# A squared-ReLU trunk on one core: a second block of each MLP up product computed with the input standing still, and PSUM taken in pairs of banks

## The chip, the cores and the metric

The kernel runs on one core of a Trainium2 chip. Its engines have short names in the profile: PE (TensorE, matmuls), PEld (its weight loads), DVE (VectorE), ACT (ScalarE), POOL (GpSimd) and SP (SyncE, whose queue carries the weight DMAs here). The metric is the device time of one execution in microseconds (us), lower is better; the number compared is the median of several runs.

## The reference

Two layers work on 256 tokens of 2048 channels, in float32. Layer 0 mixes tokens with a convolution module, layer 1 with latent attention. Each is followed by the MLP that the change is about:

```
def rms_norm(x, g):
    y = xf * lax.rsqrt(jnp.mean(xf * xf, axis=-1, keepdims=True) + NORM_EPS)
    return (y * g).astype(x.dtype)

def sq_relu_mlp(h, w1, w2):
    return jnp.square(jax.nn.relu(h @ w1)) @ w2

h = rms_norm(x, norm_mlp_g[layer])
x = x + sq_relu_mlp(h, mlp_w1[layer], mlp_w2[layer])
```

The weight `mlp_w1` is 2048 x 8192 and `mlp_w2` is 8192 x 2048. A final norm follows layer 1.

## The kernel before, in words

**Three products for one.** Each float32 number is split into an upper part that TensorE's fast float32r form holds exactly (`hi`, a copy by ScalarE) and the rest (`lo`, a subtraction by VectorE). A product is hi x hi + lo x hi + hi x lo, three matmuls (`mm3`, L202 to 206). Weights come by DMA into `raw` (three buffers), are split into `hi` and `lo` tiles (`upper_half` L165, `lower_half` L174, six buffers each) and are used once, so that VectorE and ScalarE work a few units ahead of TensorE and no further.

**The MLP** (`mlp`, L624) goes through the 8192 hidden columns in two halves (`hf`). A half is an up product into eight groups `g` of 512 columns, then a down product from them into the 2048 channels. The activations of group `g` stay in SBUF as `gh`/`gl` (or `sh`/`sl`) tiles.

**The up product has two forms.** In the form with the weight standing still (L754 to 765) 128 x 128 blocks of the weight are the stationary operand, and the input of all 256 tokens moves past: one matmul of 512 columns takes `hi` of the weight against both parts of the input side by side (`xt`), one of 256 columns takes `lo` of the weight against the input's upper part. A group is 128 matmuls in four units of four k-blocks, into four PSUM banks; the result is channel-major, as the down product wants it. The group's close (L776 to 787) adds the two halves of each bank, squares the positive part, multiplies by the square of the norm's scale (`r2_row`) and splits the result.

In the form with the input standing still (`up_block`, L697) the input's 128 x 128 blocks are stationary and 512 weight columns move. There the 2 x 2 blocks of a pair of k-blocks can be multiplied with seven products in the place of eight (`Sums.mixed` L551, Strassen's method as Winograd wrote it): 21 matmuls for a pair and not 24 (`Sums.plain`, L564). Seven combinations of weight blocks are made by `mixed_weights` (L491), seven of the input by `up_forms` (L650, tiles `fh`/`fl`). The sums need eight banks: four that are results (`e`) and four that are joined at the end (`u`, by `parts`, L587). The result is token-major: it is scaled and made positive by ScalarE (L715), turned by 16 transposes on TensorE (L724), squared (L727) and split. The turning is kept back and run among the matmuls of the group behind the block (`late`, L768).

Before the change a half runs the groups 0 to 3 with the weight standing still, then one block for the groups 4 and 5, then 6 and 7 (`UP_AT = 4`). Of the block's eight pairs the pairs 1, 2, 3 and 4 are mixed, in the order 0, 1, 2, 5, 3, 4, 6, 7; its plain pairs take their stationary operand from `xt`.

**The down product** (L788 on) has the activations stationary and the weights moving, with seven or eight of its sixteen pairs mixed (`MIXED`, L44), in two sweeps of 1024 columns with the eight banks changing roles.

**What sets the order.** The convolution and the attention are in an order written out by hand. In the MLP a planner orders each engine's instructions by their place in the program and by when it thinks that they are ready; TensorE's matmuls come in the order of the program. A PSUM or SBUF tile is given out again when all that read it are done.

Of the kernel before, what the change touches and what calls it, by code (L numbers as in the profile page):

```python
# [80 lines left out]
def trunk_kernel(  # L81
# [33 lines left out]
    psum, psum_cx = {}, [ExitStack()]  # L115

    def repool(name, **banks):

        psum_cx[0].close()
        psum_cx[0] = ExitStack()  # L120
        psum.clear()
        for kind, n in banks.items():
            psum[kind] = psum_cx[0].enter_context(tc.tile_pool(name=kind + name, bufs=n, space=PSUM, reuse_waits="tile"))
# [21 lines left out]

    def acc_tile():
        return psum["acc"].tile([P, NB], F32, tag="acc", name=nm("acc"))
# [372 lines left out]
    def mixed_inputs(v, fh, fl):  # L520

        def halves(src, at, n):
            hi, lo = fh[:, at : at + n, :], fl[:, at : at + n, :]
# [3 lines left out]
        a = v.rearrange("p k (t n) -> p (k t) n", t=T)  # L529
        a11, a21, a12, a22 = (a[:, i, :] for i in range(4))  # L530
        halves(a[:, 0:1, :], 0, 1)
        halves(a[:, 2:4, :], 1, 2)
        mixed_sums(a11, a21, a12, a22)
        halves(a, 3, 4)

    class Sums:


        def __init__(self, n, by_dma, swap=None):
            self.n, self.by_dma = n, by_dma  # L540
            ps = [acc_tile() for _ in range(8)]
            e, self.u = (ps[:4], ps[4:])[:: -1 if (n > 0 if swap is None else swap) else 1]
            self.e = [e[2 * t : 2 * t + 2] for t in range(T)]
# [80 lines left out]
    def mlp(layer, ssq, next_gain, finish=None, before=None, beside=None, after_up=None):  # L624

        with ExitStack() as cx:
# [4 lines left out]
            r2_row = mp.tile([P, S], F32, name=nm("r2_row"))  # L631
            repool(f"mlp{layer}", acc=8)

            def v_tile():
                return mp.tile([P, 2, S], F32, tag="v", name=nm("v"), bufs=4)

            def room():
                return v_tile().rearrange("p a n -> p (a n)")

            def scales():  # L640
                r = rms_rstd(ssq[:, :, :NNB], NNB, D, "n")
                r2 = small.tile([P, T], F32, tag="r2", name=nm("r2"))
                nc.vector.tensor_tensor(r2, r, r, op=ALU.mult)
                o = [acc_tile() for _ in range(4)][0]
                for t in range(T):
                    nc.tensor.transpose(o[:, t * P : (t + 1) * P], r2[:, t : t + 1].broadcast_to([P, P]), ident)
                nc.scalar.activation(r2_row, o[:, :S], AF.Copy)
                return r

            def up_forms(i, fs):  # L650

                p, v = UP_MIXED[i], v_tile()
                xp = xt[p // 2][:, 2 * p % 4 : 2 * p % 4 + 2, :].bitcast(F32)
                nc.vector.tensor_tensor(v, xp[:, :, :S], xp[:, :, S:], op=ALU.add)
                a = v.rearrange("p k (t n) -> p (k t) n", t=T)
                a11, a21, a12, a22 = (a[:, j, :] for j in range(4))
                mixed_sums(a11, a21, a12, a22)
                h, l = (f[i // 2][:, i % 2, 3:, :] for f in fs)
                nc.scalar.activation(h, a, AF.Copy)
                nc.vector.tensor_tensor(l, a, h.bitcast(F32), op=ALU.subtract)  # L660
                for c, f in enumerate(fs):
                    o = f[i // 2][:, i % 2]
                    nc.scalar.activation(o[:, 0, :], xp[:, 0, c * S : c * S + P], AF.Copy)
                    nc.scalar.activation(o[:, 1:3, :], xp[:, 1, c * S : (c + 1) * S].rearrange("p (t n) -> p t n", t=T), AF.Copy)

            def up_form(k, fs):

                i = UP_MIXED.index(k // 2)
# [6 lines left out]
            def activations(g, b2, v):  # L675

                gh, gl = gs[g]
                if 2 * g + b2 in ms:
                    mixed_inputs(v, gh[:, b2], gl[:, b2])
                    return  # L680
                if g in mixed:
                    v = v.rearrange("p k (t n) -> p (k t) n", t=T)
                    h, l = gh[:, b2, : 2 * T, :], gl[:, b2, : 2 * T, :]
                else:
                    h, l = (a[:, 2 * b2 : 2 * b2 + 2, :] for a in (gh, gl))
                nc.scalar.activation(h, v, AF.Copy)
                nc.vector.tensor_tensor(l, v, h.bitcast(F32), op=ALU.subtract)
# [9 lines left out]
            def up_block(hf, g, fs, temps):  # L697
# [3 lines left out]
                left = [p for p in UP_ORDER if p in UP_MIXED]  # L701
                for p in UP_ORDER:
                    if p in UP_MIXED:
                        left.remove(p)
                        sums.mixed(mlp_w1[layer], 2 * p, up_form(2 * p, fs), not left)
                        continue
                    end = p == UP_ORDER[-1]
                    if end:
                        parts = sums.parts(*temps)
                    sums.plain(mlp_w1[layer], 2 * p, xh_kt, xl_kt, 2 * p, end)  # L710
                for c in range(2):
                    for t in range(T):
                        z = parts[t, c]
# [1334 lines left out]
```

## Time and profile before

| | |
|---|---|
| median of 3 runs | 1932.62 us (1932.3 to 1933.16) |
| the profiled execution: its own time | 1932.2 us |
| its span, first to last instruction | 1930.4 us |
| PE / PEld busy | 99% / 86% of the span |
| DVE / ACT / POOL busy | 87% / 59% / 13% |
| HBM read over the span | 189 GB/s |

The profile is of one execution. A row of the groups gives line, engine, operation, output and inputs, count, busy time and mean duration; a row of the windows gives a stretch from the span's start, its length, and the busy time and number of instructions of each engine in it (an instruction that reaches in from outside is counted too). The ends of matmuls are modelled, and a matmul's row overlaps the next one's: what a matmul costs is read from the length of a stretch with a known number of them.

### The profile page before, as it was taken

Reading aid. Unit: us, or ns where it says so; the run is one execution under the profiler, and the core shown is the slowest. Engines: PE = TensorE matmul, PEld = TensorE weight load, DVE = VectorE, ACT = ScalarE, POOL = GpSimd, SP = SyncE. Lnnn points to the kernel's source line nnn. Section 1 sums busy time; section 2 is a strip of 40 time slices with the busy share of each in tenths; the row PEclk is TensorE's granted clock in tenths of the full one; section 3 lists DMA queues with packets and bytes.
Section 4 is the critical chain, followed back from the end, with each engine's and each line's share of the span. In section 5 each row is a group of like instructions: output and inputs, shape, how many; then the busy total and the mean of one; then the engine's idle time right before and its main releaser. Section 6 shows DMA issues by size and latency. Waiting matters only on the chain.

```text
span 1930.4 us, 28294 instructions
## 1 busy us (share of the span) xinstructions
PE 1916.9 (99%) x10485; PEld 1665.0 (86%) x10485; DVE 1675.8 (87%) x2602; ACT 1147.1 (59%) x1752; POOL 248.7 (13%) x208
## 2 busy tenths in 40 slices
PE   9999999999999999999999999999999999999998
PEld 8999888888888888888898998888888888888887
DVE  7999989997989789799976765898889988888998
ACT  5667756565555655655576655565655556565554
POOL 6999200000010100000001420000000010000000
PEclk9999999999999999999999999999999999999999
DMA  7766455656585865655656545464646686465774
GB/s 230 214 183 189 153 188 189 212 175 197 177 247 198 249 211 172 208 175 197 218 173 178 142 132 187 162 212 158 220 162 222 217 249 220 163 228 175 231 219 150
DMA packets 222235, 375.48 MB, mean 195 GB/s; under 512 B 16392, under 2 KB 107792, under 8 KB 221840
## 3 DMA queue, kind: packets, MB, share of 16 engines
q1 hardware_dynamic: 216448, 363.28, 57.6%
q0 software_dynamic: 4320, 7.87, 2.2%
q10 hardware_dynamic: 1328, 2.52, 0.4%
q8 instruction: 82, 1.34, 0.3%
q14 instruction: 57, 0.47, 0.1%
HBM read 363.68 MB, written 2.10 MB: 189 GB/s over the span
## 4 chain that ended last, share of the span: by engine, by line
PE 96%; DVE 2%; DMA 0%; issue 0%; ACT 0%; ACTq 0%; DVEq 0%
PE acc L764 18%; PE acc L206 18%; PE acc L204 18%; PE acc L205 18%; PE acc L765 10%; PE acc L925 8%; PE acc L1389 2%; DVE sum L1012 1%; DMA xs<-in_x 0%; PE acc L1637 0%; PE acc L1666 0%; PE acc L1668 0%; PE acc L1638 0%; PE acc L1639 0%; PE acc L1667 0%; PE tr L268 0%
## 5 line engine op out<-in xcount | busy, mean ns | idle before, releaser
L171 ACT ACTIVATE hi<-raw 128x1024 fp32r<-128x1024 f32 (+2 forms) x542 | 545.8, 1032 | 235.9 <-PE acc L764 105.8
L175 DVE TENSOR_TENSOR lo<-raw,hi 128x1024 fp32r<-128x1024 f32 (+2 forms) x477 | 560.6, 1194 | 127.9 <-ACT hi L171 120.9
L764 PE MATMUL acc<-xt,hi 128*128 128x512 f32 x1536 | 534.3, 391 | 0.0
L498 ACT ACTIVATE hi<-raw 128x1024 fp32r<-128x1024 f32 (+1 forms) x312 | 288.2, 948 | 303.4 <-DVE raw L506 164.7
L765 PE MATMUL acc<-xt,lo 128*128 128x256 f32 x1536 | 433.0, 282 | 0.0
L499 DVE TENSOR_TENSOR lo<-raw,hi 128x1024 fp32r<-128x1024 f32 (+1 forms) x312 | 332.6, 1087 | 45.0 <-ACT hi L498 40.3
L764 PEld LDWEIGHTS acc<-xt,hi 128*128 128x128 f32 x1536 | 288.3, 188 | 60.4
L765 PEld LDWEIGHTS acc<-xt,lo 128*128 128x128 f32 x1536 | 290.3, 189 | 0.3
L204 PE MATMUL acc<-hi,sh 128*128 128x512 f32 x514 | 200.1, 389 | 0.0
L206 PE MATMUL acc<-lo,sh 128*128 128x512 f32 x514 | 200.0, 389 | 0.0
L204 PE MATMUL acc<-hi,gh 128*128 128x512 f32 (+1 forms) x516 | 200.0, 388 | 0.0
L205 PE MATMUL acc<-hi,gl 128*128 128x512 f32 (+1 forms) x516 | 199.9, 387 | 0.0
L206 PE MATMUL acc<-lo,gh 128*128 128x512 f32 (+1 forms) x516 | 199.9, 387 | 0.0
L925 PE MATMUL acc<-xt,hi 128*128 128x256 f32 x1024 | 180.2, 281 | 0.3 <-ACT b L1208 0.2
L205 PE MATMUL acc<-hi,sl 128*128 128x512 f32 x450 | 175.1, 389 | 0.0
L583 POOL DMA_DIRECT2D xs<-v x30 | 26.3, 957 | 1135.4 <-DVE lo L175 701.9
L1012 DVE SCALAR_TENSOR_TENSOR sum<-ub,w_dw,sum 128x256 f32<-128x256 f32 x409 | 164.4, 485 | 3.6 <-ACT sum L982 3.0
L175 POOL TENSOR_TENSOR lo<-raw,hi 128x1024 fp32r<-128x1024 f32 x65 | 154.8, 2404 | 17.2 <-ACT hi L171 17.2
L925 PEld LDWEIGHTS acc<-xt,hi 128*128 128x128 f32 x1024 | 154.6, 188 | 1.1 <-ACT xt L1192 0.6
L925 PE MATMUL acc<-xt,lo 128*128 128x256 f32 x512 | 139.2, 279 | 0.0
L206 PEld LDWEIGHTS acc<-lo,gh 128*128 128x128 f32 x516 | 96.9, 188 | 19.9
L204 PEld LDWEIGHTS acc<-hi,gh 128*128 128x128 f32 x516 | 96.9, 188 | 19.7
(342 smaller groups left out, 3083.6 us busy)
## 6 DMA issues: line engine op xcount, KB each, us to landing
raw<-in_mlp_w SPq DMA_DIRECT2D x255, 1024.0 KB, 5.5
raw<-in_conv_w_pw SPq DMA_DIRECT2D x62, 512.0 KB, 5.1
raw<-in_conv_w_pw SPq DMA_DIRECT2D x16, 1024.0 KB, 5.0
raw<-in_mla_w_o SPq DMA_DIRECT2D x16, 1024.0 KB, 5.3
raw<-in_mla_w_kv_up SPq DMA_DIRECT2D x32, 256.0 KB, 3.9
xs<-v POOLq DMA_DIRECT2D x30, 256.0 KB, 7.6
raw<-in_mla_w_in SPq DMA_DIRECT2D x8, 576.0 KB, 3.7
raw<-in_mla_w_in SPq DMA_DIRECT2D x4, 1024.0 KB
```

The costliest lines, as they stand in the source:

```text
L171: nc.scalar.activation(hi, raw[:, js, :], AF.Copy)
L175: eng.tensor_tensor(lo, raw, hi.bitcast(F32), op=ALU.subtract)
L204: nc.tensor.matmul(ps, sh, mh, start=start, stop=False)
L205: nc.tensor.matmul(ps, sl, mh, start=False, stop=False)
L206: nc.tensor.matmul(ps, sh, ml, start=False, stop=stop)
L498: nc.scalar.activation(hi, src, AF.Copy)
L499: nc.vector.tensor_tensor(lo, src, hi.bitcast(F32), op=ALU.subtract)
L764: nc.tensor.matmul(ps[b], wh[:, bs], xhl(k), start=k == 0, stop=False)
L765: nc.tensor.matmul(ps[b][:, :S], wl[:, bs], xh(k), start=False, stop=k == KC - 1)
L925: nc.tensor.matmul(pss[c][b][:, :S], w[i][:, bs], (xh, xl)[j](k), start=k == i + j == 0, stop=end and k == k0 + nk - 1 and (i, j) == terms ...
L1012: nc.vector.scalar_tensor_tensor(out=out, in0=ubs[c][:, w : w + S], scalar=tap(c, w), in1=base, op0=ALU.mult, op1=ALU.add)
L1389: nc.tensor.matmul(ps2[b][t], x_kt(k, t), w[:, bs], start=k == g == i == 0, stop=k == KC - 1 and i == len(group) - 1,)
```

## The change

- Each half of an up product now has two blocks with the input standing still, for the groups 0 and 1 and for 2 and 3; the groups 4, 5, 6 and 7 keep the weight standing still. The order is 4, 5, block, 6, block, 7 (`UP_PLAN`). The mixed pairs of the down product move to the groups 0 to 3; their number stays.
- The mixed pairs of a block are 2, 3, 4 and 5, in the order 0, 2, 3, 1, 4, 5, 6, 7. Both blocks of a half use the same input forms, made once, two pairs by one call.
- The plain pairs take the input from copies of `xt[0]` and `xt[3]`, made by ScalarE into buffers that later hold activations (`up_copies`). The second block has the copy of `xt[3]` only; the buffer of the other is needed by then.
- PSUM in the MLP is given out in pairs of banks (`pair_tile`). A group's close is one copy and one addition of two banks each, one instruction for positive part and scale, a square by ScalarE, and the split, each over 1024 elements. The scale is that of the norm (`r_row`), the small tiles `r2` are gone, and it is turned by TensorE inside the last unit of the first group rather than behind it.
- The sums of a block are joined and made positive two banks at a time; the 16 transposes of a block run in one piece, and its squares and splits are twice as wide.
- The tables of the rotary embedding (`beside`) are made in layer 0's second half, not its first. At the start of the attention four small writes that touch PSUM tiles come behind the first three products.

```diff
-MIXED = {(layer, half): (0, 1, 4, 5, 8, 9, 12) + (13,) * (layer + half < 2) for layer in range(2) for half in range(2)}
+MIXED = {(layer, half): tuple(range(7 + (layer + half < 2))) for layer in range(2) for half in range(2)}
-UP_AT, UP_ORDER, UP_MIXED = 4, (0, 1, 2, 5, 3, 4, 6, 7), (1, 2, 3, 4)
+UP_PLAN, UP_ORDER, UP_MIXED = (4, 5, 0, 6, 2, 7), (0, 2, 3, 1, 4, 5, 6, 7), (2, 3, 4, 5)
+UP_FORMS = ({(1, 1): 0, (1, 3): 1}, {(0, 2): 0, (1, 1): 1})
+UP_COPIES = ({(1, 0): 0, (1, 2): 3}, {(1, 0): 0, (1, 2): 3})
...
+    def pair_tile():
+        return psum["pair"].tile([P, 2, NB], F32, tag="pair", name=nm("pair"))
...
-            repool(f"mlp{layer}", acc=8)
+            repool(f"mlp{layer}", pair=4)
...
-                r2 = small.tile([P, T], F32, tag="r2", name=nm("r2"))
...
+            def up_copies(n):
+                for c, a in enumerate(copied[n]):
+                    nc.scalar.activation(a, xt[n].bitcast(F32)[:, :, c * S : (c + 1) * S], AF.Copy)
...
-                for c in range(2):
-                    for t in range(T):
-                        z = parts[t, c]
-                        nc.vector.tensor_tensor(z, sums.e[t][c], z, op=ALU.add)
-                        nc.scalar.activation(z, z, AF.Relu, scale=r_cols[0][:, t : t + 1])
+                for t, z in enumerate(zs):
+                    o = z.rearrange("p (c n) -> p c n", c=2)
+                    nc.vector.tensor_tensor(o, sums.pe[t], o, op=ALU.add)
+                    nc.scalar.activation(z, z, AF.Relu, scale=r_cols[0][:, t : t + 1])
...
-                for g in range(ng):
-                    if g == UP_AT:
-                        late = up_block(hf, g, fs, temps)
-                    if g in (UP_AT, UP_AT + 1):
+                for nth, g in enumerate(UP_PLAN):
+                    if g in mixed:
+                        late = up_block(hf, g, fs, {n: a for n, a in copied.items() if nth < 3 or n > 0})
                         continue
-                    ps = [acc_tile() for _ in range(4)]
+                    pairs = [pair_tile() for _ in range(2)]
+                    ps = [a[:, b, :] for a in pairs for b in range(2)]
...
-                    if beside is not None and g == 2:
-                        beside(mp)
+                    if beside is not None and hf == nth == 1:
+                        beside(v_tile())
...
-                    for b2 in range(2):
-                        v = v_tile()
-                        for b in range(2):
-                            o = ps[2 * b2 + b]
-                            nc.scalar.activation(v[:, b, :], o[:, S:], AF.Copy)
-                            nc.vector.tensor_tensor(v[:, b, :], o[:, :S], v[:, b, :], op=ALU.add)
-                        nc.vector.scalar_tensor_tensor(out=v, in0=v, scalar=0.0, in1=v, op0=ALU.max, op1=ALU.mult)
-                        row = r2_row.rearrange("p (a n) -> p a n", a=1).broadcast_to([P, 2, S])
-                        nc.vector.tensor_tensor(v, v, row, op=ALU.mult)
-                        activations(g, b2, v)
+                    v = v_tile()
+                    for i, a in enumerate(pairs):
+                        vi = v[:, 2 * i : 2 * i + 2, :]
+                        nc.scalar.activation(vi, a[:, :, S:], AF.Copy)
+                        nc.vector.tensor_tensor(vi, a[:, :, :S], vi, op=ALU.add)
+                    row = r_row.rearrange("p (a n) -> p a n", a=1).broadcast_to([P, 4, S])
+                    nc.vector.scalar_tensor_tensor(out=v, in0=v, scalar=0.0, in1=row, op0=ALU.max, op1=ALU.mult)
+                    nc.scalar.activation(v, v, AF.Square)
+                    activations(g, v)
...
-            for o in (ps[1][0], free[4]):
-                nc.vector.memset(o[:, 0:1], 0.0)
-            nc.scalar.activation(ps[1][1][:, 0:1], ident[:, 0:1], AF.Copy)
-            nc.vector.memset(free[5][:, 0:1], 0.0)
...
                         if k == t == 0 and i == 1:
-                            nc.scalar.activation(ps[1][0][:, 0:1], ident[:, 0:1], AF.Copy)
+                            for o in free[4:]:
+                                nc.vector.memset(o[:, 0:1], 0.0)
+                            for o in ps[1][::-1]:
+                                nc.scalar.activation(o[:, 0:1], ident[:, 0:1], AF.Copy)
```

More of the change, by code (lines that the diff above doesn't have):

```diff
@@ L143, in nm @@
         return f"{s}_{uid[0]}"
+    def pair_tile():
+        return psum["pair"].tile([P, 2, NB], F32, tag="pair", name=nm("pair"))
     def acc_tile():
+        if "pair" in psum:
+            if not spare:
+                both = pair_tile()
+                spare.extend(both[:, i, :] for i in range(2))
+            return spare.pop(0)
         return psum["acc"].tile([P, NB], F32, tag="acc", name=nm("acc"))
@@ L704, in up_block @@
                         left.remove(p)
-                        sums.mixed(mlp_w1[layer], 2 * p, up_form(2 * p, fs), not left)
+                        sums.mixed(mlp_w1[layer], 2 * p, up_form(p, fs), not left)
                         continue
@@ new lines, in up_block, with turned @@
+                        sums.parts(*(z[:, c * NB : (c + 1) * NB] for z in zs for c in range(2)))
+                    sums.plain(mlp_w1[layer], 2 * p, at_kt(0), at_kt(1), 2 * p, end)
+                for t, z in enumerate(zs):
+                    o = z.rearrange("p (c n) -> p c n", c=2)
+                    nc.vector.tensor_tensor(o, sums.pe[t], o, op=ALU.add)
+                    nc.scalar.activation(z, z, AF.Relu, scale=r_cols[0][:, t : t + 1])
+                def turned():
+                    pts = [a.rearrange("p b (k t n) -> p (b k) t n", t=T, n=P) for a in sums.pe]
+                    for c in range(2):
+                        for f in range(4):
```

153 lines of the change are left out of this document (81 added, 72 removed).

## The prediction

> **What bounds the kernel now.** First the page: which engine is full, at what clock, and what the chain that ended last consists of.
>
> ```profile
> PE 1916.9 (99%) x10485; PEld 1665.0 (86%) x10485; DVE 1675.8 (87%) x2602; ACT 1147.1 (59%) x1752; POOL 248.7 (13%) x208
> PEclk9999999999999999999999999999999999999999
> PE 96%; DVE 2%; DMA 0%; issue 0%; ACT 0%; ACTq 0%; DVEq 0%
> ```
>
> TensorE is the bound: 96% of the chain, full clock in every slice. A gain has to be fewer or shorter matmuls; a loss, a wait of TensorE that isn't there now. VectorE, at 87%, is the engine that could cause one. Next the windows, all engines, over layer 0's second half: groups 0 to 3, the block, groups 6 and 7; then the down product of the half before.
>
> ```profile
> 640.66:729.42 88.76, 88.76 (x513) 78.67 (x512) 72.33 (x119) 50.43 (x83) 1.77 (x2) 1.00 0.67 216
> 729.42:771.14 41.72, 41.72 (x182) 33.66 (x181) 39.81 (x48) 24.17 (x29) 0.00 (x0) 1.00 0.53 182
> 771.14:817.28 46.14, 46.14 (x274) 41.08 (x273) 35.92 (x60) 29.00 (x46) 0.00 (x0) 1.00 0.66 213
> 477.42:640.66 163.24, 163.24 (x723) 135.18 (x721) 151.43 (x163) 91.97 (x104) 8.86 (x10) 1.00 0.65 208
> ```
>
> TensorE has no gap in any of them. One group with the weight standing still costs 88.76 / 4 = 22.19 us. Two of them, 44.4 us, are what a block replaces; a block takes 41.72. VectorE is busy 95% of the block (39.81 of 41.72) and 93% of the down product, and TensorE doesn't wait for it. The block cut at its changes of form, TensorE alone, with a batch of eight transposes, a later down stretch of 30 matmuls with the stationary operand `oh`, and one of 12 with `kvh`:
>
> ```profile
> 729.42:735.02 5.60, 5.60 (x27) 1.00 0.36 112
> 735.02:744.55 9.53, 9.53 (x43) 1.00 0.15 52
> 750.15:759.94 9.79, 9.79 (x43) 1.00 0.32 110
> 759.94:771.14 11.20, 11.20 (x49) 1.00 0.94 299
> 409.95:420.07 10.12, 9.98 (x43) 1.00 0.34 113
> 782.24:783.03 0.79, 0.79 (x11) 1.00 1.01 368
> 1217.46:1224.26 6.80, 6.80 (x31) 1.00 0.45 147
> 1040.21:1043.01 2.80, 2.80 (x14) 1.00 0.07 19
> ```
>
> By the code a plain pair is 24 matmuls and two mixed pairs are 42. So a matmul from `xt` costs 5.60 / 24 = 233 ns, one from the forms `fh`/`fl` 9.53 / 42 = 227 ns, one of the down product, from `gh`/`sh`, 163.24 / 720 = 226.7 ns. The second mixed run is 0.26 us longer than the first, and in the first block of all (10.12) by 0.59: there the combinations of weight blocks come a little late. Which buffer is stationary is worth 6.5 ns: `oh` 227, `kvh` 233, same width and clock.
>
> **The change part by part.** The four up halves are the place of nearly all of it:
>
> ```profile
> 300.22:477.42 177.20, 177.06 (x968) 1.00 0.58 191
> 640.66:817.28 176.62, 176.62 (x966) 1.00 0.64 207
> 1241.04:1417.95 176.91, 176.91 (x968) 1.00 0.58 191
> 1581.16:1757.78 176.62, 176.62 (x965) 1.00 0.64 207
> ```
>
> They add to 707.35 us. A half after the change:
>
> - Four groups with the weight standing still: 4 x 22.19 = 88.76.
> - First block: 84 mixed and 96 plain matmuls. The plain ones read copies that lie in the buffers of `gh`/`gl`, from which the down product runs at 226.7, so 180 x 0.2267 = 40.81. Second block: 48 of its plain matmuls still read `xt`: 132 x 0.2267 + 48 x 0.2333 = 41.12.
> - The present block has 0.28 us beyond its matmuls (41.72 less 96 x 0.2333 + 84 x 0.2267 = 41.44). I keep that for each block: 0.56.
> - Transposes: 32 for 16, 4 x 0.79 = 3.16. The two turnings of today leave 46.14 - 2 x 22.19 - 1.58 = 0.18 at their edges; two batches: 0.18.
>
> Sum 174.59; four halves and 0.4 for the turning of the scale (a pair of transposes in each layer) 698.8. **The gain is 8.5 us.** The rest lies beside other work:
>
> *VectorE.* Its rows, whole run:
>
> ```profile
> L175 DVE TENSOR_TENSOR lo<-raw,hi 128x1024 fp32r<-128x1024 f32 x449 | 540.6, 1223 | 123.4 <-ACT hi L171 116.5 <-PE tr L268 2.6 <-PE acc L206 2.4
> L499 DVE TENSOR_TENSOR lo<-raw,hi 128x1024 fp32r<-128x1024 f32 x234 | 284.0, 1222 | 45.0 <-ACT hi L498 40.3
> L499 DVE TENSOR_TENSOR lo<-raw,hi 128x512 fp32r<-128x512 f32 x78 | 53.4, 684 | 0.0
> L506 DVE TENSOR_TENSOR raw<-raw 128x1024 f32<-128x1024 f32 x78 | 95.1, 1220 | 0.4
> L507 DVE TENSOR_TENSOR raw<-raw 128x512 f32<-128x512 f32 x78 | 53.9, 691 | 2.3
> L783 DVE TENSOR_TENSOR v<-acc,v 128x256 f32<-128x256 f32 x96 | 37.1, 421 | 0.3 <-ACT v L782 0.3
> L784 DVE SCALAR_TENSOR_TENSOR v<-v 128x512 f32<-128x512 f32 x48 | 32.9, 685 | 0.4
> L786 DVE TENSOR_TENSOR v<-v,r_row 128x512 f32<-128x512 f32 x48 | 32.9, 685 | 0.0
> ```
>
> A mixed pair costs 3 x 1.22 + 0.68 + 1.22 + 2 x 0.69 = 6.95 us of VectorE against 21 x 0.227 = 4.8 of TensorE; a plain pair 2.45 against 5.4. A block's weights are 4 x 9.4 = 37.6, its joining 4 x 0.69 + 2 x 1.22 = 5.2. A group's weights are 8 x 1.22 = 9.8. Its close was 4 x 0.42 + 4 x 0.69 + two splits of 0.69 = 5.8; now 2 x 0.69 + 1.22 + 1.22 = 3.8. The forms of a block's two groups cost about 2 x (0.42 + 0.69 + 4 x 0.42 + 1.22) = 8. A block and the group behind it: 37.6 + 5.2 + 9.8 + 3.8 + 8 = 64.4 of TensorE's 41.4 + 22.2 + 1.6 = 65.2, 99%. That looks fatal, but rows overlap. The down product by the same rows has 2 x 8 x 9.4 = 150.4 for weights and some 10 for joining and closing, 98% of its 163.24; the window shows 151.43 busy and no wait. So I take no more waiting than today, on thin cover: were the weights late by a whole 0.59 in every run, it would cost the price under the second rival.
>
> *ScalarE.*
>
> ```profile
> L498 ACT ACTIVATE hi<-raw 128x1024 fp32r<-128x1024 f32 x234 | 245.3, 1057 | 288.9 <-DVE raw L506 164.7 <-DVE raw L508 44.9 <-PE acc L206 21.8
> ```
>
> At 1.06 us for 1024 elements, per half: four more mixed pairs 4 x 1.5 of them, 6.4; copies 4.2; squares of four groups 4.2; joining, relu and squares of a second block about 5, less the closes of two groups, about 4. That is 16 us on 50.43 + 24.17 + 29.00, 68% of the half. It hides behind TensorE while VectorE is the later engine.
>
> *The scale.* The transposes move some 2.8 us ahead of the first group's end, and the groups behind them on TensorE wait for `r`:
>
> ```profile
> 316.90 0.16 DVE L643 TENSOR_TENSOR r<-y 128x2 f32<-128x2 f32 x1
> 322.42 0.38 PE L646 MATMUL acc<-ident,r 128*128 128x128 f32 x2
> ```
>
> `r` is there 5.5 us early, so nothing is lost. The rotary tables go from a half with the forms to one without the norm's work; no queue of DMAs is passed.
>
> *Start of the attention.* TensorE waits there for the last close:
>
> ```profile
> PE acc L204 <- DVE xs L616: 1.3, 1, 1.3
> ```
>
> The moved writes let three products go first, but a pair of banks comes free only when both are closed: between 1.3 gained and 1.3 lost. I take nothing.
>
> So the profiled execution's 1932.2 us (span 1930.4) becomes 1923.7; the median of the runs is 0.4 above that execution: 1924.
>
> [...]
>
> **The rivals.**
>
> 1. *The stationary buffers move to the slow side (slower).* The trace says that some buffers cost 233 ns and others 227, not why; `kvh` and `oh` have alike shapes, and the same weights move past them. If it is where a buffer begins, the removal of the `r2` tiles, in a pool that is laid out ahead of the MLP's and the attention's, shifts all that have 227. About 2886 down matmuls and 672 mixed ones would cost 6.5 ns more, 23.1 us, and the 576 from copies lose their 3.7; `oh` and the convolution's, 768 of them, add 5.0: 1924 + 32 = 1956. It ends slower once the shift costs more than about 2 ns for each. Against: nothing shows that a shift so small has any effect. Chance 0.18.
>
> 2. *VectorE is late in every block (no change).* Two mixed pairs in a row need 13.9 us of VectorE, and the two runs quoted above were late by 0.26 and 0.59. If each of the 16 runs is late by 0.59, 9.4 for the 2.2 counted, the time is 1931. For: the 99% above, and that a block now has only one group behind it. Against: shorter closes, and the down product. Chance 0.08.
>
> 3. *A group waits for the pair that it just filled (no change).* A copy of 512 and an addition, 0.6 + 0.7 us for each pair, at each of four places where one group follows another: up to 2 us each, 1932. For it speaks that two banks come free together. Against:
>
> ```profile
> 322.56 0.48 PE L764 MATMUL acc<-xt,hi 128*128 128x512 f32 x1
> 324.84 0.42 DVE L783 TENSOR_TENSOR v<-acc,v 128x256 f32<-128x256 f32 x1
> ```
>
> the second group begins at 322.56, though the first one's last bank is closed at 325.26 only, so a group takes banks that are free. Chance 0.04.
>
> [...]
>
> **How the numbers follow.** 0.2% is 3.9 us, about what a measurement of this kernel can tell from no change. The forecast, 0.70: 1924, from 1920.5 (no pauses, 2.2 less, and the attention's wait gone) to 1928.7. Rivals 2 and 3, 0.12, end within 0.2%. Rival 1, 0.18, is slower. The range that leaves out rival 1 alone is 1920.5 to 1932. If the copies run at 233 after all, the time is 1928, inside it.
>
> **What would show it.** Right: plain pairs of 5.44 us in the first block and 5.60 for pairs 0 and 1 in the second, blocks of 41.1 and 41.4, halves of 174.6, a batch of 16 transposes in 1.6, DVE about 88%, no new line among TensorE's waits. Wrong: down products longer than 163.2 with no wait (rival 1); second mixed runs above 10 us (rival 2); a gap between the first two groups (rival 3).

## The result: slower by 18.5 us, and the profile after

| | before | after |
|---|---|---|
| median of 4 runs | 1932.46 us | 1950.99 us (1949.5 to 1951.48) |
| ratio of the runs, 95% interval | | 1.0094 (1.0077 to 1.0112) |
| the profiled execution's span | 1930.4 us | 1949.6 us |

The forecast was 1924, the range 1920.5 to 1932: the result lies 27 us above the one and 19 above the end of the other. From the page of the changed kernel, the lines that answer to the prediction's first three:

```profile
PE 1928.1 (99%) x10245; PEld 1654.1 (85%) x10245; DVE 1694.4 (87%) x2382; ACT 1192.6 (61%) x1655; POOL 248.7 (13%) x208
PEclk9999999999999999999999999999999999999998
PE 86%; DVE 10%; ACT 2%; issue 2%; DMA 0%; DVEq 0%; ACTq 0%
```

TensorE runs 240 matmuls fewer, as intended, and is busy for longer. Its share of the chain falls from 96 to 86%; VectorE has 10% of it, against 2. TensorE's three longest waits in the changed kernel follow (the line that waits, what it waited for, us in total, times, longest). The first two aren't in the kernel before; the third is:

```profile
PE pair L215 <- ACT hi L509: 4.5, 9, 0.7
PE pair L215 <- DVE xs L400: 3.9, 2, 3.4
PE acc L1133 <- POOL ident masks.py:199: 1.6, 1, 1.6
```

The windows of the changed kernel, all engines: the four up halves, the down product of layer 0's first half, the last down product, and the two mixed runs of a second block. Below them the last down product of the kernel before:

```profile
301.81:479.35 177.54, 176.43 (x906) 149.80 (x907) 158.24 (x195) 116.55 (x140) 0.00 (x0) 1.00 0.54 186
644.17:822.09 177.92, 176.29 (x905) 149.37 (x904) 155.62 (x199) 114.45 (x132) 1.76 (x2) 1.00 0.61 202
1248.67:1426.47 177.80, 176.48 (x908) 149.66 (x907) 158.44 (x197) 116.87 (x140) 0.00 (x0) 1.00 0.54 187
1591.49:1768.45 176.96, 175.85 (x905) 149.46 (x904) 151.55 (x172) 112.12 (x129) 1.89 (x3) 1.00 0.62 205
479.35:644.17 164.82, 164.82 (x722) 135.22 (x721) 152.69 (x159) 94.65 (x107) 8.81 (x10) 1.00 0.65 210
1768.45:1941.84 173.39, 169.50 (x740) 138.75 (x738) 151.65 (x175) 93.61 (x116) 5.21 (x6) 0.98 0.59 190
417.61:428.63 11.02, 10.19 (x43) 7.73 (x42) 10.56 (x12) 7.68 (x9) 0.00 (x0) 1.00 0.29 98
434.23:444.42 10.19, 9.91 (x43) 7.81 (x42) 9.97 (x11) 7.02 (x8) 0.00 (x0) 1.00 0.33 113
```

```profile
1757.78:1922.67 164.89, 164.89 (x740) 136.84 (x738) 151.27 (x179) 91.97 (x116) 5.24 (x6) 1.00 0.60 198
```

Three things are to be read here. The down product of 720 matmuls takes 164.82 in place of 163.24 and TensorE waits for nothing in it: each matmul costs 228.9 ns, not 226.7. The mixed runs have 42 matmuls, 9.6 us at that rate; they take 11.02 and 10.19, with TensorE idle for a part and VectorE full (10.56 of 11.02, 9.97 of 10.19). And the last down product, 164.89 before, is 8.5 us longer, with idle time and a clock of 0.98. By stages, from the first matmul of one to the first of the next (the last column is the best version found below):

| us | before | forecast | after | by columns |
|---|---|---|---|---|
| to the first MLP | 300.22 | 300.2 | 301.81 | 300.89 |
| four up halves | 707.35 | 698.8 | 710.22 | 701.55 |
| four down products | 651.83 | 651.8 | 665.30 | 653.29 |
| attention | 263.27 | 263.3 | 264.51 | 264.67 |
| behind the last matmul | 7.73 | 7.7 | 7.76 | 8.00 |

### The profile page after: what moved, and what is told of

It reads as the page before. It is cut to its first block, busy times and chain, and to the rows that moved or that the text cites. A ratio compares the mean times of both kernels' runs of the same rounds, so it can differ in the third digit from the quotient of the medians.

```text
span 1949.6 us, 27537 instructions
## 1 busy us (share of the span) xinstructions
PE 1928.1 (99%) x10245; PEld 1654.1 (85%) x10245; DVE 1694.4 (87%) x2382; ACT 1192.6 (61%) x1655; POOL 248.7 (13%) x208
## 4 chain that ended last, share of the span: by engine, by line
PE 86%; DVE 10%; ACT 2%; issue 2%; DMA 0%; DVEq 0%; ACTq 0%
PE pair L215 15%; PE pair L217 15%; PE pair L216 14%; PE pair L796 10%; PE acc L955 8%; PE pair L797 6%; PE acc L215 4%; PE acc L217 4%; PE acc L216 4%; PE acc L1419 2%; DVE lo L510 2%; DVE sum L1042 1%; DVE raw L517 1%; ACT hi L509 1%; DVE sl L538 1%
## 5 line engine op out<-in xcount | busy, mean ns | idle before, releaser
L509 ACT ACTIVATE hi<-raw 128x1024 fp32r<-128x1024 f32 x376 | 347.3, 948 | 320.5 <-DVE raw L517 191.8
L510 DVE TENSOR_TENSOR lo<-raw,hi 128x1024 fp32r<-128x1024 f32 x376 | 400.5, 1087 | 33.8 <-ACT hi L509 28.6
L796 PE MATMUL pair<-xt,hi 128*128 128x512 f32 x1024 | 357.2, 391 | 0.4 <-DVE pair L779 0.2
L797 PE MATMUL pair<-xt,lo 128*128 128x256 f32 x1024 | 288.6, 282 | 0.0
L796 PEld LDWEIGHTS pair<-xt,hi 128*128 128x128 f32 x1024 | 192.2, 188 | 41.2 <-issue 0.6
L215 PE MATMUL pair<-hi,gh 128*128 128x512 f32 (+1 forms) x516 | 203.5, 394 | 3.9 <-DVE xs L400 3.9
L217 PE MATMUL pair<-lo,gh 128*128 128x512 f32 (+1 forms) x516 | 202.4, 392 | 0.0
L216 PE MATMUL pair<-hi,gl 128*128 128x512 f32 (+1 forms) x516 | 200.7, 389 | 0.0
L797 PEld LDWEIGHTS pair<-xt,lo 128*128 128x128 f32 x1024 | 193.5, 189 | 0.5
L955 PEld LDWEIGHTS acc<-xt,hi 128*128 128x128 f32 x1024 | 154.6, 188 | 1.2 <-ACT xt L1222 0.8
L955 PE MATMUL acc<-xt,lo 128*128 128x256 f32 x512 | 139.2, 279 | 0.0
```

The lines of the kernel that those rows point to most:

```text
L215: nc.tensor.matmul(ps, sh, mh, start=start, stop=False)
L216: nc.tensor.matmul(ps, sl, mh, start=False, stop=False)
L217: nc.tensor.matmul(ps, sh, ml, start=False, stop=stop)
L796: nc.tensor.matmul(ps[b], wh[:, bs], xhl(k), start=k == 0, stop=False)
L797: nc.tensor.matmul(ps[b][:, :S], wl[:, bs], xh(k), start=False, stop=k == KC - 1)
L955: nc.tensor.matmul(pss[c][b][:, :S], w[i][:, bs], (xh, xl)[j](k), start=k == i + j == 0, stop=end and k == k0 + nk - 1 and (i, j) == terms ...
```

## Where the operands begin

Theory A: the vanished `r2` tiles took 64 bytes out of the pool `small`, all that is laid out behind it begins 64 bytes earlier, and a stationary operand's start sets the price of a matmul. By the program's own layout `gh`, `sh`, `fh` and `oh` began at a multiple of 128 bytes before, `xt` and `kvh` 32 bytes behind one; the moving weights lie ahead of that pool and keep their places. Theory B: pairs and wide instructions slow the reading. First the 64 bytes given back, and the same 64 taken from the kernel before:

```diff
-PAD_SMALL = 48    # the changed kernel, after_pad
+PAD_SMALL = 64
-PAD_SMALL = 48    # the kernel before, before_less64
+PAD_SMALL = 32
```

> The changed kernel with 64 bytes of padding more in the pool `small`, so that everything laid out behind it begins where it began before the change. Theory A (the vanished `r2` tiles moved the stationary operands by 64 bytes, and that alone made each matmul of 512 columns 2.2 ns longer): the down products go back from 228.9 to 226.7 ns for each matmul, 163.2 us instead of 164.8; the convolution ends at 300.2 instead of 301.8; with 1.6 there, 4 x 1.6 in the down products, 1.3 in the attention and 4 x 312 x 2.2 ns in the blocks that is 12 us, so 1939. Theory B (the pairs of banks or the wider instructions slow TensorE's reading): 228.9 stays, and 1951 with it. Neither touches the waits in the second blocks or the one at the end.

> The kernel before with 64 bytes of padding less in the pool `small` and nothing else changed. Theory A: the same 2.2 ns for each 512-column matmul with a stationary operand behind that pool, without any of the change's other parts: down products 164.8 instead of 163.2, convolution 1.6 later, 1932.5 + 1.6 + 6.5 + 1.3 + about 1 in the blocks = 1943. Theory B: 1932.5, unchanged.

Measured: 1944.92 (ratio to before 1.0064, 1.0049 to 1.0079) and 1939.21 (1.0033, 1.002 to 1.0047). One down product of each, the padded kernel's from layer 1, the unchanged kernel's with 64 bytes less from layer 0:

```profile
1423.49:1587.05 163.56, 163.56 (x723) 135.08 (x721) 150.69 (x158) 93.33 (x107) 7.77 (x9) 1.00 0.65 209
```

```profile
478.24:643.05 164.81, 164.81 (x722) 135.23 (x721) 152.86 (x164) 92.90 (x104) 8.88 (x10) 1.00 0.65 208
```

The 226.7 ns came back (163.2 is 720 of them, the rest is a late weight), and 228.9 can be made in a kernel that has nothing else of the change: theory B falls. The shift is worth 6.6 us in the kernel before (four down products 1.6 each) and 6.1 in the changed one. I had expected 12 there. Of that, 2.7 should have come in the blocks, where a faster TensorE only met late weights (the mixed runs add to 164.7 us with the padding, 163.2 without). Some 1.9 are missing in the convolution and the down products, which fell by less than 1.6 each (the first of them from 164.82 to 163.82). And 1.3 were expected in the attention, which has 264.6 with the padding and 264.5 without. The traces show two changes there that cancel: from the first product with `kvh` on, it takes 207.4 us in both kernels with the shift and 206.4 in both without, while the stretch ahead of that product, 56.8 in the kernel before, has 57.1 in the changed kernel and 58.2 with the padding.

But the prediction had read 6.5 ns off the trace, and this is 2.2. Does the 6.5 belong to other distances?

```diff
-PAD_SMALL = 48    # the kernel before
+PAD_SMALL = 40    # before_less32; before_less96 has 24
```

> The kernel before with 32 bytes of padding less in the pool `small`, where 64 less cost 6.6 us. Theory A1 (each 32 bytes has a price of its own, and the 6.5 ns that the trace of before shows for `xt` and `kvh` belongs to this one): down products at 233 ns for each matmul, 167.9 us instead of 163.2, 6.5 ns x (2886 + 672 + 768) = 28 us more, less what `kvh` may win: 1955 to 1961. Theory A2 (any shift off the present place costs the same 2.2 ns): 1939 to 1943. Theory A3 (only a shift of 64 matters): 1932.5.

> The kernel before with 96 bytes of padding less in the pool `small`. Theory A1: as for 32 bytes, since 96 is as far from the next multiple of 128: 233 ns, 1955 to 1961. Theory A2: 1939 to 1943. If the price grows with the distance: above the one of 32 bytes less.

Measured: 1956.32 (1.0124, 1.0095 to 1.0154) and 1954.75 (1.0116, 1.0087 to 1.0146), two runs each. The same down product in both, 32 bytes less and 96 bytes less:

```profile
479.85:647.83 167.98, 167.98 (x722) 134.96 (x721) 153.77 (x165) 93.21 (x104) 8.90 (x10) 1.00 0.64 205
```

```profile
480.30:648.30 168.00, 168.00 (x722) 135.16 (x721) 153.74 (x165) 93.29 (x104) 8.84 (x10) 1.00 0.64 205
```

233.3 ns in both. So the start within 128 bytes has three prices here: 226.7 at 0, 228.9 at 64, 233.3 at 32 and 96. At 32 bytes less `kvh` comes to begin at 0, and its matmuls fall from 233 to about 230, not to 226.7: the three prices don't cover it. What was still to be shown is that `xt` can be made faster, in the best version below:

```diff
-PAD_RIGHT = 48
+PAD_RIGHT = 56    # cols_xt; cols_xt_kv has PAD_KV 32 for 8 and PAD_O 32 for 56 as well
```

> The column version with 32 bytes of padding more ahead of `xt`, so that `xt` too begins at a multiple of 128. Theory A1 (the start of the stationary operand within 128 bytes sets the price, for every buffer): the matmuls that load `xt` fall from 233 to 227 ns: 192 in the second blocks and 480 of the attention's, 672 x 6.5 ns = 4.4 us, 1925.5. Rival (it is a property of `xt` for another reason, such as the three uses that it has): 1930. A loss is open where `xt` moves past the weights in the groups, 1024 matmuls of 512 columns and as many of 256: had its place been good for that, each ns there would cost 1 us.

> The same, and the padding of the attention's pool set so that `kvh` and what lies beside it begin at a multiple of 128 as `oh` does. Theory A1: the 96 matmuls of 512 columns with `kvh` or `kvl` standing still fall from 233 to 227 ns, 0.6 us less than the last one. Rival: no change, or a loss where the same tiles are read by other engines or move.

Measured: 1937.63 (1.0027, 1.0016 to 1.0037) and 1938.88 (1.0032, 1.002 to 1.0045), 8 and 9 us slower than the version they start from, 1929.91. (`cols_xt` moves some operands of the attention too; that stage changes by less than 0.2.) The windows show why: a stretch of the first groups, where `xt` moves (144 matmuls), and a plain pair of a second block, where it stands still. First the version by columns, then `cols_xt`:

```profile
320.52:345.57 25.05, 25.05 (x147) 22.20 (x146) 22.71 (x28) 19.62 (x25) 0.00 (x0) 1.00 0.52 179
410.77:416.37 5.60, 5.60 (x27) 4.52 (x25) 5.53 (x7) 3.97 (x6) 0.00 (x0) 1.00 0.38 118
```

```profile
325.58:351.09 25.51, 25.51 (x147) 22.13 (x146) 23.07 (x28) 19.64 (x25) 0.00 (x0) 1.00 0.50 171
416.19:421.67 5.48, 5.48 (x26) 4.51 (x25) 5.41 (x7) 3.84 (x6) 0.00 (x0) 1.00 0.37 108
```

Standing still, `xt` gained what theory A says: 5.48 for 5.60, its 192 matmuls in the second blocks at 227.4 ns and not 233.2. Moving, it lost: 0.46 us in this stretch, and the convolution, where it moves in 1536 matmuls, ended 4.7 us later (305.58 against 300.89). So theory A holds for `xt` too where it is stationary, as for the activations and the forms; the better place for the moving `xt` is the one it had. For `kvh` theory A is not borne out: beginning at 0 in `cols_xt_kv`, its matmuls take 232.4 ns on average, 232.9 before, and no gain in time can be seen. What sets its price stays open.

## Weights that come late into the second block

Theory A3: VectorE comes late into the second block because the turned first block's sums and splits, issued behind the second quarter of group 6, are still queued. VectorE's rows in the changed kernel just ahead of the run of 11.02 (start, us, engine, line):

```profile
408.89 1.22 DVE L538 TENSOR_TENSOR sl<-v,sh 128x1024 fp32r<-128x1024 f32 x1
410.03 0.42 DVE L529 TENSOR_TENSOR v<-v 128x256 f32<-128x256 f32 x1
410.37 0.68 DVE L510 TENSOR_TENSOR lo<-raw,hi 128x512 fp32r<-128x512 f32 x1
410.97 1.22 DVE L517 TENSOR_TENSOR raw<-raw 128x1024 f32<-128x1024 f32 x1
412.10 1.22 DVE L538 TENSOR_TENSOR sl<-v,sh 128x1024 fp32r<-128x1024 f32 x1
```

`sl` is the turned block's, wanted only by the down product at 479; the rows L510 and L517 are the second block's first mixed weights. That TensorE's wait names ScalarE's `hi` is no objection, for ScalarE itself waits for VectorE's `raw` there; its longest wait between 400 and 440 us:

```profile
ACT hi L509 <- DVE raw L517: 8.9, 3, 3.2
```

The edit, first in the padded kernel with single banks at its end (next section), then alone:

```diff
-                        if late and u > 0:
+                        if late and (u > 0 or nth == 3):
```

> The last one, and the first block's turning issued after the first quarter of the group behind it instead of after the second, 5.6 us earlier. Theory A3 (VectorE comes late into the second block because the turned block's mixed sums and splits, begun late, are still queued ahead of that block's weight combinations): the second blocks' first mixed run falls from 11.0 to about 9.7 and the second from 10.2 towards 9.7, 1.3 to 1.8 us for each half, 5 to 7 in all, 1926. Rival (VectorE's work over block and group exceeds their time, wherever it is put): the first run improves and the second takes it back, under 2 us in all; or TensorE waits for the relu at the earlier turning.

> The changed kernel with the first block's turning one quarter of a group earlier, and nothing else: no padding, pairs of banks at the end as they are. Theory A3 (the three causes are separate and add): second blocks without waits, the runs at 9.6, 1951.0 less the 9.2 that the same edit took from the padded kernel: 1942, with 228.9 ns for a matmul and the 3.8 us gap at the end still there. Rival (the earlier turning only paid because the padding had made TensorE faster and VectorE the limit): less than 5, above 1946.

Measured: 1933.47 (1.0004, 0.9994 to 1.0013), 9.2 less than the 1942.72 without the edit; alone 1942.45 (1.0051, 1.0036 to 1.0066), 8.5 less than the changed kernel. Theory A3 holds, and the effect doesn't hang on the padding. The second block's two runs and the whole block, in the first of the two kernels:

```profile
416.37:425.90 9.53, 9.53 (x43) 7.88 (x42) 8.31 (x9) 6.58 (x8) 0.00 (x0) 1.00 0.19 56
431.49:441.05 9.56, 9.56 (x43) 7.88 (x42) 9.34 (x11) 6.39 (x8) 0.00 (x0) 1.00 0.34 115
410.77:451.93 41.16, 41.16 (x182) 33.79 (x181) 39.37 (x42) 25.51 (x29) 0.00 (x0) 1.00 0.55 189
```

9.53 and 9.56 are 42 matmuls with nothing between them. VectorE still has 39.37 of 41.16 in it: not the load of the block was too high, but the backlog at its start.

## The wait at the end, and the clock behind it

Theory A2: two banks of a pair are one buffer to the program, so that a matmul into one waits for a read of the other. In the last down product each pair held a sum of one column and a sum of the next. TensorE there in the changed kernel, and VectorE at the same time:

```profile
1909.69 0.40 PE L217 MATMUL pair<-lo,gh 128*128 128x512 f32 x1
1913.45 0.76 PE L215 MATMUL pair<-hi,gh 128*128 128x512 f32 x1 [3.37 <-DVE xs L400]
1914.02 0.63 PE L216 MATMUL pair<-hi,gl 128*128 128x512 f32 x1
1914.44 0.63 PE L217 MATMUL pair<-lo,gh 128*128 128x512 f32 x1
```

```profile
1909.62 0.69 DVE L618 TENSOR_TENSOR v<-pair,v 128x512 f32<-128x512 f32 x1
1910.22 0.68 DVE L619 TENSOR_TENSOR v<-pair,v 128x512 f32<-128x512 f32 x1
1910.82 1.89 DVE L598 TENSOR_TENSOR xs<-v,xs 128x512 f32<-128x512 f32 x3
1912.62 1.28 DVE L400 TENSOR_TENSOR xs<-pair,xs 128x512 f32<-128x512 f32 x2
```

The next column's first matmul begins when the first of the two additions L400, which read the column just finished, is done; they stand behind VectorE's joining. Behind the gap the matmuls start 427 ns apart for some 5 us: the gap of 3.8 us costs 3.5, the slow clock 2.6 more, and a second gap, of 0.8 us between the two halves of the last sum, 0.6. The granted clock in the 8 us around it was 0.63 on average (the third number from the end):

```profile
1910.00:1918.00 8.00, 4.63 (x12) 3.61 (x12) 7.44 (x12) 5.68 (x14) 0.00 (x0) 0.63 0.60 213
```

Three remedies, the first in the padded kernel, the other two with the earlier turning as well:

```diff
+                    repool("end", acc=8)                       # pad_end: single banks in a new pool
...
-                    sums = Sums(NNB - 2, False)
+                    sums = Sums(NNB - 2, False, swap=False)    # tail2: and other banks first;
...
+        if "pair" in psum:                                     # a pair for each turned column block
+            return pair_tile()[:, 0, :]
...
+            self.e = [[a[:, 0, :], b[:, 0, :]], [a[:, 1, :], None]]    # cols: by column, no new pool;
+            self.e[1][1] = pair_tile()[:, 0, :]                         # the last sum's pair taken later
```

> The padded kernel, and the last two column blocks of the final down product again in eight single banks instead of four pairs. Theory A2 (in the last down product TensorE waits because the two banks of a pair count as one buffer: the next column's matmuls wait until VectorE has read the other bank): the gap of 3.8 us and that of 0.8 go, and with the first the 5 us of matmuls at 427 ns behind it: 3.5 + 2.6 + 0.6 = 6.7 less, 1932. Rival (VectorE is late there for its own work, as it is in the second blocks): the wait stays under another name, within 1 us of the padded kernel.

> Padding, single banks at the end, earlier turning, and two more places where a matmul waits for a bank: the final product begins in the four banks that the product before freed first, and each transposed column block between the MLP and the attention gets a pair of its own instead of one bank of a shared pair. Theory: the gap of 2.6 us at the start of the final product goes (2.4) and so does the 1.0 before the transposes at the attention's start: 1933.5 less 3.4, 1930. Rival (these waits stand for VectorE and ScalarE being late with closing, whichever banks are taken): 1933, under 1 us.

> The changed kernel with the padding, with the earlier turning, and with the final product's sums laid over its pairs of banks by column: both sums of the first column in one pair, those of the second in two others, each half of the last sum in a pair of its own. No pool is opened anew. Theory A2 (what TensorE waits for at the end is a read of the other bank of the same pair): no gap above 0.4 us between the columns, none between the halves, full clock there, the last down product 165 to 165.5 us instead of 167.4 in the kernel with single banks in a new pool: 1931. Rival (VectorE's joining is late there, whatever bank is taken): a gap of 1 to 3 us remains and 1933.5 with it.

Measured, in this order: 1942.72 (1.0051, 1.0036 to 1.0066), 2.2 less than the padded kernel and not 6.7; 1934.31 (1.0012, 1.0002 to 1.0021), no gain over 1933.47; 1929.91 (0.9986, 0.9976 to 0.9996), 3.6 less than 1933.47. The new pool brought a wait of its own, for the close of the sweep before; this is `pad_end`:

```profile
PE pair L215 <- ACT hi L509: 6.0, 14, 0.7
PE acc L215 <- ACT v L633: 2.2, 1, 2.2
```

Eight matmuls 427 ns apart, 1.6 us more than at full clock, follow that wait too, so that the last down product still has 169.0 us. In `tail2` the same wait has 2.3, whichever banks come first, which points to the pool's change and not to a bank; the transposes' wait of 1.0 stayed too. By columns the last down product is what it was before the change, without a gap:

```profile
1755.57:1920.45 164.88, 164.83 (x739) 136.78 (x738) 151.32 (x176) 93.03 (x116) 5.23 (x6) 1.00 0.62 200
```

So theory A2 holds. This version (padding, earlier turning, sums by column) is below the kernel before, by 0.14%.

## What the second block is worth, and VectorE in the first

`one_block` is `tail2` with the groups 2 and 3 with the weight standing still again:

```diff
-UP_PLAN, UP_ORDER, UP_MIXED = (4, 5, 0, 6, 2, 7), (0, 2, 3, 1, 4, 5, 6, 7), (2, 3, 4, 5)
+UP_PLAN, UP_ORDER, UP_MIXED = (4, 5, 0, 6, 2, 3, 7), (0, 2, 3, 1, 4, 5, 6, 7), (2, 3, 4, 5)
-                    if g in mixed:
+                    if g == 0:
```

> The kernel with padding, banks, turning and transposes mended, but with one block in each half, as before the change: the groups 2 and 3 with the weight standing still again. It shows what the second block is worth by itself. By rows: 2 groups, 44.4 us, against 41.0 and the 1.7 of its transposes: 1.7 for each half, 7 us over four: 1937 if the mended one has 1930. Rival (the second block costs VectorE what it saves TensorE): within 2 us of the mended kernel.

Measured: 1941.32 (1.0046, 1.0031 to 1.0061), 7.0 more than `tail2`. The second blocks bring what the rows said; in the traced executions 6.1 of it lie in the halves and 1.2 in the last down product, whose code is the same.

What is left in the halves lies in the first blocks, whose runs take 9.5 to 10.5 us. Theory A4: VectorE's load. Four edits on it, one to `tail2` and three to the version by columns (`cols_order` also splits the last plain pair ahead of the joining):

```diff
-    nc.vector.tensor_tensor(gl, v, gh.bitcast(F32), op=ALU.subtract)      # gps: gl, the last sl,
+    nc.gpsimd.tensor_tensor(gl, v, gh.bitcast(F32), op=ALU.subtract)      # and the forms' fl
...
-UP_FORMS = ({(1, 1): 0, (1, 3): 1}, {(0, 2): 0, (1, 1): 1})
+UP_FORMS = ({(0, 1): 0, (0, 3): 1}, {(0, 1): 0, (0, 3): 1})               # cols_forms
-UP_PLAN, UP_ORDER, UP_MIXED = (4, 5, 0, 6, 2, 7), (0, 2, 3, 1, 4, 5, 6, 7), (2, 3, 4, 5)
+UP_PLAN, UP_ORDER, UP_MIXED = (4, 5, 0, 6, 2, 7), (0, 1, 2, 3, 6, 4, 5, 7), (2, 3, 4, 5)  # cols_order
-                    if beside is not None and hf == nth == 1:
+                    if beside is not None and hf == 0 and nth == 1:       # cols_rotary
```

> The last one, and the low halves of the activations and of the forms (not those of the weights) subtracted on GpSimd, which is idle there, instead of VectorE. Theory A4 (what is left in the first blocks, runs of 10 to 10.9 us instead of 9.5, is VectorE's load of nearly 100% there): some 8 instructions of 1.2 us in a half leave VectorE, the runs fall to 9.5 to 9.6, about 1 us for each of four halves and the 1 to 1.6 us of gaps in two down products: 5 less than the last one, 1925. Rival (the chain is one of latency, from a split to the sums behind it, and GpSimd's 2.4 us for 1.2 makes it longer, or the two engines hinder each other): no better or up to 5 worse.

Measured: 1971.93 (1.0204, 1.0189 to 1.0219), 37.6 more than `tail2` and not 5 less. GpSimd's row and VectorE's at the start of a first block:

```profile
355.00 2.61 POOL L702 TENSOR_TENSOR gl<-v,gh 128x1024 fp32r<-128x1024 f32 x1 [14.20 <-ACT gh L701]
```

```profile
354.67 0.69 DVE L512 TENSOR_TENSOR lo<-raw,hi 128x512 fp32r<-128x512 f32 x1
355.39 2.77 DVE L520 TENSOR_TENSOR raw<-raw 128x512 f32<-128x512 f32 x1
358.08 1.21 DVE L512 TENSOR_TENSOR lo<-raw,hi 128x1024 fp32r<-128x1024 f32 x1
```

VectorE's L520, 0.69 us otherwise, began while GpSimd ran (355.00 to 357.61) and ended 0.55 behind it: it came to its end only when GpSimd's instruction was over. At 31 of the 41 subtractions moved, an instruction of VectorE that began beside GpSimd's ended 0.55 us (512 elements) or 1.08 (1024) behind it. In eight cases VectorE's first subtraction beside it kept its 1.22 us and GpSimd's took longer instead, 4.0 us or more for 2.4; an addition of VectorE with one input in PSUM (L816) kept its 0.68. So one subtraction moved over costs VectorE up to 2 us and not 1.2 less. Why the two engines hold each other up, no run shows.

> The same, with the input forms of the blocks made in the first group of each half instead of the second (in the first layer half) or the first and second. Theory A4 (VectorE comes into the first block behind because the forms, about 8 us of it, fall in the group right ahead): the runs of the first block fall from 9.9 and 10.4 to 9.6, 0.3 to 1.5 us a half, 3 in all: 1928. Rival (VectorE has caught up by the block's beginning, and only the block's own load counts): no change, 1931.

> The column version, and the rotary tables made in the first half of layer 0 again, as before the change. Theory: they are why the first block of layer 0's second half is the worst (first run 10.9 us, the others 9.5 to 9.9); it falls to 9.9, the one in the first half rises by as much: no change in the sum, 1931. If they only cost where the half also has late forms, 1 less: 1930.

> The column version, and in each block two plain pairs ahead of the mixed ones and one more between them, (0, 1, 2, 3, 6, 4, 5, 7); the last plain pair is split ahead of the joining. VectorE needs 2.4 us for a plain pair and 6.9 for a mixed one, TensorE 5.4 and 4.8. Theory A4 (VectorE's load in a row of mixed pairs): each run of two starts with 3 us more in hand, all runs 9.5, 3 to 4 us less, 1927. Rival (VectorE is at its limit over the whole block, so the wait only moves to the joining and to the group that needs the joined banks): 1931 or later, with a new wait at the group behind the block.

Measured: 1935.61 (1.0014, 1.0005 to 1.0024), 1930.85 (0.9991, 0.9982 to 1.0001) and 1936.53 (1.0021, 1.0011 to 1.003), against 1929.91. With the forms in the first group TensorE waits for the norm's scale, 2.1 us in two places, and the first blocks of the second halves become worse, not better. The rotary tables are what makes layer 0's second half the worst: moved, its first run falls from 10.38 to 9.52, and the first half's rises from 9.52 to 10.23, no gain in the sum. The order with two plain pairs ahead shows both blocks without any wait:

```profile
345.16:385.97 40.81, 40.81 (x182) 33.79 (x181) 38.02 (x41) 24.91 (x28) 0.00 (x0) 1.00 0.51 177
411.35:452.47 41.12, 41.12 (x182) 33.79 (x181) 37.80 (x40) 24.99 (x28) 0.00 (x0) 1.00 0.50 174
```

40.81 and 41.12 are the prediction's sums to the digit. And yet it is 6.6 us slower, since the joining now ends behind the block, and the group and the turning wait for it:

```profile
PE pair L810 <- DVE v L619: 3.4, 8, 0.7
PE pair L763 <- ACT v L755: 2.0, 4, 0.7
```

The expectation's rival holds: over a block and what follows it the wait only moves.

## Why the prediction was wrong, step by step

By the table of stages the profiled execution lies 27.8 us above the forecast: 13.5 in the down products, 11.4 in the halves, 1.6 ahead of the first MLP and 1.2 in the attention.

- **The halves' sum, 698.8.** The terms were right: blocks of 40.81 and 41.12 where nothing waits, 16 transposes in 1.66 for the 1.6, a second block worth 7.0 us. What failed is "no more waiting than today, on thin cover". The 16 mixed runs of the changed kernel add to 163.2, 9.4 above 16 x 9.61, where the forecast had kept 2.2. That this is rival 2's own 16 x 0.59, which had 0.08, is chance: rival 2 had every run late, from VectorE's load, and 8.0 of the 9.4 lie in the eight runs of the second blocks. The load of 99% was worked out and then set aside because the down product has 98% without a wait. But the block begins with a backlog, and the down product doesn't: VectorE took the turned block's splits in between the second block's first weights. The edit that moves them gives 8.5 to 9.2 us.
- **Rival 1, 0.18.** Its condition was true, its price was not: 6.5 ns was read off `xt`, which begins 32 bytes behind a multiple of 128; the shift was of 64, for which the runs show 2.2 ns. 6.1 us, not 32. At 2.2 ns the rival's own sum, some 4900 matmuls, is 10.8, and with it alone the time would have been 1935, not 1951. It was known from the change that the tiles go, and the chance should have been higher.
- **The last down product.** It was not in the working at all. Pairs of banks were weighed for the groups (rival 3, "it just filled", which didn't come: the waits at the groups' L796 are 0.4 us in all) and for the attention's start. The same mechanism, at a place where one pair holds sums of two columns, costs 3.5 + 0.6 us of waits and 2.6 of slow clock.
- **The attention, "I take nothing" between 1.3 gained and 1.3 lost.** 1.2 lost. 1.0 of it is the shift (207.4 us for 206.4 from the first product with `kvh` on), a part of rival 1, and 0.2 the start. With the padding the 1.0 comes back and the start loses 1.4, the worst that the prediction gave. Most of that is waiting for VectorE's `xt`, 2.0 us in two places, where the kernel before waited 1.3 in one. The two in the padded kernel:

```profile
PE acc L215 <- DVE xt L228: 1.1, 1, 1.1
PE pair L279 <- DVE xt L228: 1.0, 1, 1.0
```

A pair for each transposed block (`tail2`) didn't remove the second, so why `xt` is late stays open. Open too are 0.7 in the convolution, whose code is unchanged: 0.4 of it lies ahead of its first product.

- **ScalarE and the scale** cost nothing that can be seen: ACT has 61%, the waits that name its `hi` are waits for VectorE's `raw`, and no wait of TensorE names the scale as the change has it. (`r` was 5.5 us ahead of the old place of the turning, so some 2.7 ahead of the new one.)

In medians, from 1950.99: padding 6.1, earlier turning 9.2, the end 2.2 + 3.6, makes 1929.9. From there to the forecast 6 us are missing; by the table's stages 2.7 in the halves (1.3 of it in the first blocks' runs, beyond the 2.2 that the forecast had kept), 1.5 in the down products, 1.4 at the attention's start, 0.7 ahead of the MLP.

## What to carry to other kernels

Ask of a change that frees or adds a small tile what is laid out behind it (64 bytes were worth 6.1 and 6.6 us here), and measure one padded version before the rest is judged. Where an engine is nearly full, look at what stands in its queue at a stretch's start and not only at its load over the stretch: with the turning moved, VectorE had 39.37 of a block's 41.16 us and TensorE didn't wait; so issue what is wanted late well ahead of that stretch. And where banks are joined into one buffer, go through every place that reads one half while the other is written (3.5 + 0.6 us of waits here).

## What the runs showed of the hardware that was not expected

- The start of a stationary operand within 128 bytes: 226.7 ns at 0 (the kernel before), 228.9 at 64 (the changed kernel), 233.3 at 96 (`before_less32`) or 32 (`before_less96`), for 512 columns, in the down product. At 64, in the changed kernel, the three matmuls of a product differ (232, 226 and 229 ns for hi x `gh`, hi x `gl`, lo x `gh`). `kvh` doesn't follow it: 230.0 (`before_less32`) and 232.4 (`cols_xt_kv`) at 0, 232.9 at 32 (the kernel before).
- Moving, `xt` did better 32 bytes behind the multiple: 229.6 ns in the groups of the version by columns, 235.5 at 0 in `cols_xt` (233.9 in `cols_xt_kv`, where it begins at 0 as well); in the convolution, at 256 columns, 116.7 and 120.0 in the same two.
- Gaps shorter than the 3.8 us above were followed by slow matmuls too: in `cols_forms` a gap of 1.7 us and one of 0.9 were followed, 3.8 us behind the start of the first, by seven matmuls 427 ns apart. The length of the gap alone doesn't tell it: in `pad_end_late` a gap of 2.6 us brought none, in `pad_end` one of 2.6 brought eight, in `tail2` one of 2.7 six.
- In `gps` a VectorE instruction of 0.69 us took 2.77 beside one of GpSimd, and in eight cases GpSimd's of 2.4 took 4.0 or more beside one of VectorE.
